# Two changes to a one-core diffusion trunk: the adaLN scale of layer 0 as products on PE, and gate tiles placed behind the key and query projections

## The chip, the cores and the metric

The kernel runs on one core of a Trainium2 chip. The core has five engines with instruction streams of their own: PE (TensorE, matrix products), DVE (VectorE), ACT (ScalarE), POOL (GpSimd) and SP (SyncE, which issues most of the DMA transfers). The metric is the time of one execution on the device in microseconds (us). Three runs of the kernel before took 2922.29, 2915.41 and 2922.88 us, a median of 2922.29 us. The one execution that was profiled took 2915.37 us.

## The reference

The reference is a trunk of two layers over 256 context tokens and 1024 latent tokens of 1024 features (`D`). Each layer mixes tokens and then runs a squared-ReLU MLP. Layer 0 mixes by multi-head latent attention, layer 1 by a bidirectional gated linear attention (GLA). Cut to what the change touches:

```python
m_lat = silu(c)     @ ada_w[i] + ada_b[i]      # 6 rows of D: shift, scale, gate, shift, scale, gate
m_ctx = silu(c_ctx) @ ada_w[i] + ada_b[i]
h_lat = rms_norm(x_lat, norm_g[i, 0]) * (1 + m_lat[1]) + m_lat[0]
h_ctx = rms_norm(x_ctx, norm_g[i, 0]) * (1 + m_ctx[1]) + m_ctx[0]
# layer 0: h_all (context, then latent) goes into
cq, ckv = h_all @ w_dq, h_all @ w_dkv          # low-rank query (384), key/value (256) and rotary key (64)
# layer 1 (GLA): h_all goes into keys, queries, values, a swish gate, and per direction d
g[d] = log_sigmoid((h_all @ w_gate1[d]) @ w_gate2[d] + b_gate[d]) / 16
```

Everything is computed in float32. The kernel gets that accuracy from PE by splitting each operand into a high and a low part and adding three products.

## The kernel before, in words

Features lie on the 128 partitions, tokens along the free dimension. A feature axis of 1024 is eight tiles, `k` = 0 to 7. Tokens form three blocks (`BLK`): 0 is the context (256 tokens), 1 and 2 are latent (512 each). `mm3` (lines 231 to 235) issues the three products of a split pair, so each of the lines 233, 234 and 235 has a third of them. A split (`split`, lines 202 to 204) is a cast on ACT (line 203) and a subtraction on DVE or POOL (line 200).

**Layer 0's inputs** (`low_rank_inputs`). The products of `w_dq` and `w_dkv` form six output tiles per token block, which are accumulated over `k` in six of the eight PSUM banks. `block` runs block 1, then 0, then 2. For block 1 the scale multiplies the weights: `first(k)` computes the latent scale of tile `k` (`ada_lat(1, k)`), scales the weight rows with it on ACT (line 425) and DVE (line 426), and loads the tokens; the tokens are split without a scale. With `ahead`, the work of step `k+1` is issued before the 18 products of step `k`. For block 0 the weights are used unscaled, and `ctx_moving` scales and shifts the tokens (lines 434 to 439), with two more columns that carry the shifts, so that the shift's share (`wb`) of the latent blocks comes out of the same products. Block 2 uses the scaled weights again.

The scale and shift of layer 0 are sums over 1024 features for each of 1024 outputs, for the latent and the context vector. In the kernel before each of the 16 tiles (`m` = 0 shift, `m` = 1 scale, `k` = 0 to 7) has one load of 512 KB into a tile named `ada` with three buffers (outputs on partitions, the 1024 summands along the free dimension). `ada_lat` multiplies it by a row of silu(c), broadcast over partitions in `cs`, and sums, in one DVE instruction (line 396). `ada_ctx` does the same with silu(c_ctx): for the six pairs in `PLAN['dve']` on DVE (line 404), for the other ten with a multiplication on POOL (line 407) and a sum on ACT (line 408). `ada_fix` adds the bias, and for a scale multiplies by the norm's weight: one DVE instruction of one column per sum (line 277 for a shift, line 282 for a scale). `PLAN['post']` and `PLAN['sec']` list what is issued after the products of step `k` of block 1 and block 0: `A` the shift or scale sums, `L` a token load, `S` a square for the norm, `T` the norm's statistics.

**Layer 1's projections** (`gla`). `PLAN['gla']` lists the order in which the items of blocks 2 and 0 run: `v` values, `s` swish gates, `h` keys and queries, `g` decay gates. Each item of `head_proj` is one projection: two weight loads, two splits, 24 products, an ACT copy, a store. `gate_items` first makes one projection of 24 products, copied to SBUF by lines 1290 to 1292; then, for each 128 tokens and each direction, a gate tile:

```python
nc.tensor.matmul(ps, st[:, j * P:j * P + P], self.gs[d], start=True, stop=True)   # 1297
nc.scalar.activation(e, ps, AF.Abs)                                               # 1299
nc.scalar.activation(e, e, AF.Exp, scale=-1.0)                                    # 1300
nc.scalar.activation(e, e, AF.Ln, bias=1.0)                                       # 1301
nc.vector.scalar_tensor_tensor(out=e, in0=ps, scalar=0.0, in1=e, ...)             # 1302
nc.sync.dma_start(self.g_scr[d, t0 // P + j], e)                                  # 1303
```

Blocks 1 and 2 have eight gate tiles, block 0 has four. The gates, keys, queries and values go to scratch in HBM, and the scan reads them back. Block 1's items are not run in `gla`: they are a chain, `fill`, of which the scan takes the next one or few between its own steps (`PLAN['pre']`, `PLAN['fill']`). The scan's first steps are context tiles, then tiles of block 2; block 1's come later. In the scan, line 1450 makes the sums of the gates (fp32 products of 130 columns) and line 1475 loads and splits the values.

**What sets the order.** Each engine runs its instructions in the order of its queue. That order is made at compile time from the program order and a simulated timeline, so an instruction can stand ahead of one that is written before it. DMA loads marked by `keep_in_program_order` (line 378 and others) keep their written order on SP's queue; a load whose buffer is not free yet holds up the queue behind it.

Of the kernel before, what the change touches and what calls it, by code (L numbers as in the profile page):

```python
# [10 lines left out]
F32 = mybir.dt.float32  # L11
F32R = mybir.dt.float32r
U8 = mybir.dt.uint8
AF = mybir.ActivationFunctionType
ALU = mybir.AluOpType
# [30 lines left out]
PLAN = {'dve': [(1, 3), (0, 7), (0, 0), (1, 2), (1, 1), (1, 7)],  # L46
 'sq': [(1, 5), (1, 7), (2, 3), (2, 7), (0, 4), (2, 4), (1, 4), (2, 1), (1, 1)],
 'xlo': [5, 7, 6, 0],
 'wlo': [7, 1, 6, 0],
# [43 lines left out]
 'gla': 'v2 s2 h2 h0 g0 v0 g2',  # L93
# [17 lines left out]
class Trunk:  # L111
    def __init__(self, ctx, tc, I, out, stop=None):
# [7 lines left out]
        def const(name, shape, dt=F32):  # L120
            return self.const.tile(shape, dt, name=name)
# [12 lines left out]
        for l in range(2):  # L134
            for s in range(2):
                for m in range(6):
                    if (l, m) == (0, 0) or l == 1 and s == 1 and m > 1:
                        continue
                    self.coef[l, s, m] = const(f"m{l}{s}{m}", [P, KT])
        self.shift0 = const("shift0", [P, KT, 2])  # L140
        for s in range(2):
            self.coef[0, s, 0] = self.shift0[:, :, s]

# [199 lines left out]
    def lay_out(self, order):  # L343

        for tag in order.split():
            if tag == "cs":
                self.cs = self.pool.tile([P, 2, D], F32, name="cs")
            elif tag == "cl":
                self.cl = self.pool.tile([P, D], F32, name="cl")
            elif tag == "junk":  # L350
                self.junk = self.pool.tile([P, D], F32, name="junk")
            else:
                self.slot(tag, 8)
# [13 lines left out]
    def low_rank_inputs(self):  # L367
# [5 lines left out]
        ada_w = {}  # L373
# [3 lines left out]
        def dma(x, src):  # L377
            self.tc.keep_in_program_order(nc.sync.dma_start(x, src))
            return x
# [14 lines left out]
        def ada_lat(m, k):  # L394
            w = dma(self.slot("ada", D), I["adaT"][0, m * KT + k])
            nc.vector.tensor_tensor_reduce(out=self.junk, in0=w, in1=self.cs[:, 0], scale=1.0, scalar=0.0,
                                           op0=ALU.mult, op1=ALU.add, accum_out=self.co(0, 0, m, k))
            self.ada_fix(0, 0, m, k)
            ada_w[m, k] = w

        def ada_ctx(m, k):
            w = ada_w.pop((m, k))
            if (m, k) in PLAN['dve']:
                nc.vector.tensor_tensor_reduce(out=w, in0=w, in1=self.cs[:, 1], scale=1.0, scalar=0.0,
                                               op0=ALU.mult, op1=ALU.add, accum_out=self.co(0, 1, m, k))
            else:
                nc.gpsimd.tensor_tensor(out=w, in0=w, in1=self.cs[:, 1], op=ALU.mult)
                nc.scalar.activation(w, w, AF.Copy, accum_out=self.co(0, 1, m, k))
            self.ada_fix(0, 1, m, k)

        def ada_lat_ctx(m, k):
            ada_lat(m, k)
            ada_ctx(m, k)
# [93 lines left out]
        def first(k):  # L507
            ada_lat(1, k)
            held[k] = weights(k, self.co(0, 0, 1, k))
            load_x(1, k)  # L510
            return held[k]
# [4 lines left out]
        def second_silu():  # L516
            self.silu(1)
            self.exp_ln_tables()
# [13 lines left out]
        fn = {"A": ada_lat_ctx, "L": load_x, "S": square, "T": stats}  # L532
        self.silu(0)
        post = {k: [(square, 1, k), (ada_ctx, 1, k)] for k in range(KT)}
        post[0].insert(0, (second_silu,))
# [711 lines left out]
    def gla(self, h):  # L1247

        nc, I = self.nc, self.I
        self.gate_weights()  # L1250
        item = {"g": lambda b: self.gate_items(h[b], b), "h": lambda b: self.head_proj(h[b], b),
                "v": lambda b: self.value_items(h[b], b, 4), "s": lambda b: self.swish_items(h[b], b)}
        for x in PLAN["gla"].split():
            b = int(x[1])
            self.ready(h[b])
            self.run(item[x[0]](b))
        x = h[1]
        self.ready(x)
        fill = chain(self.gate_items(x, 1), self.head_proj(x, 1), self.value_items(x, 1, 2), self.swish_items(x, 1))
        return self.scan(fill)  # L1260

# [20 lines left out]
    def gate_items(self, h, b):  # L1282
# [21 lines left out]
        yield  # L1304
# [297 lines left out]
def layout(i):  # L1602
# [5 lines left out]
    A["cb"] = f(np.broadcast_to(np.stack([i["c"][0], i["c_ctx"]])[None], (P, 2, D)))  # L1608
    A["adaT"] = f(i["ada_w"].transpose(0, 2, 1).reshape(2, 48, P, D))
# [53 lines left out]
```

## Time and profile before

| | us |
|---|---|
| median of three runs | 2922.29 |
| the profiled execution | 2915.37 |
| its span, first to last instruction | 2913.6 |
| PE busy in matrix products | 2746.1 (94% of the span) |
| DVE busy | 2313.1 (79%) |
| ACT busy | 1603.9 (55%) |
| POOL busy | 664.0 (23%) |

The page cuts the span into 40 slices of 73 us and gives busy time in tenths, and the clock of PE that the chip granted, in tenths of full speed:

```profile
PE   6799998999989999999999999799888999999997
...
DVE  8898899888788887798868673366898898877666
ACT  4566666666466444444545365656665644545443
...
PEclk8999999999999999999999999899999999999999
```

How to read a profile's row here: durations are in us, or in ns where the view says "mean ns"; `x16` is a count; `128x512` is partitions by elements; `out<-in` are the program's tile names (`m`, `w`, `c`, `ada`, `ps` and so on); `L396` is line 396 of the kernel. "Idle before" is the idle time of the engine just ahead of such instructions, with the instruction that ended it. A matrix product's duration includes its passage through the array, so products in a row start at closer intervals than they last. One fp32 product appears as two records. SPq is the queue in which SP issues DMA transfers.

### The profile page before, as it was taken

How to read it: one execution, taken by the hardware profiler on the slowest of the kernel's cores; microseconds unless marked ns; L12 is line 12 of the kernel's file. 1: busy time of each engine (PE TensorE's matmuls, PEld its weight loads, DVE VectorE, ACT ScalarE, POOL GpSimd, SP SyncE). 2: the span in 40 equal slices, each digit the busy share in tenths (PEclk: the TensorE clock that was granted, in tenths of full speed). 3: DMA queues.
4: the chain of work that ended last, by engine and by line, in shares of the span. 5: the costliest groups of instructions: out<-in, count | busy, mean ns of one | idle time of the engine just before them, and what ended most of it. 6: DMA issues, size and time to landing. Idle time of an engine off the chain costs nothing. (4 is left out here: it accounts for less than half of the span.)

```text
span 2913.6 us, 44354 instructions
## 1 busy us (share of the span) xinstructions
PE 2746.1 (94%) x14646; PEld 2354.7 (81%) x14646; DVE 2313.1 (79%) x4331; ACT 1603.9 (55%) x3360; POOL 664.0 (23%) x474
## 2 busy tenths in 40 slices
PE   6799998999989999999999999799888999999997
PEld 4678887898779888888887888688887778888877
DVE  8898899888788887798868673366898898877666
ACT  4566666666466444444545365656665644545443
POOL 5554444422000000000002233356561000000012
PEclk8999999999999999999999999899999999999999
DMA  5222424313646675498735465666586657677454
GB/s 201 77 77 67 129 94 143 101 61 110 230 124 233 197 250 179 163 342 285 245 122 172 166 222 161 202 218 230 189 275 213 224 195 246 203 269 259 146 178 154
DMA packets 319383, 535.47 MB, mean 184 GB/s; under 512 B 33072, under 2 KB 96432, under 8 KB 319152
## 3 DMA queue, kind: packets, MB, share of 16 engines
q1 hardware_dynamic: 313328, 527.39, 54.5%
q10 hardware_dynamic: 5760, 5.25, 0.5%
q8 instruction: 115, 1.88, 0.3%
q14 instruction: 116, 0.95, 0.1%
q0 software_dynamic: 64, 0.00, 0.0%
HBM read 412.18 MB, written 120.32 MB: 183 GB/s over the span
## 5 line engine op out<-in xcount | busy, mean ns | idle before, releaser
L234 PE MATMUL ps<-m,w 128*128 128x512 f32 (+1 forms) x2320 | 897.5, 388 | 13.2 <-DVE m L200 13.2
L233 PE MATMUL ps<-m,w 128*128 128x512 f32 (+1 forms) x2320 | 882.2, 390 | 25.2 <-ACT m L203 14.5
L235 PE MATMUL ps<-m,w 128*128 128x512 f32 (+1 forms) x2320 | 889.7, 387 | 2.1 <-DVE w L200 2.0
L200 POOL TENSOR_TENSOR w<-stg,w 128x512 fp32r<-128x512 f32 (+2 forms) x138 | 194.1, 1409 | 1706.2 <-ACT w L203 1648.3
L233 PEld LDWEIGHTS ps<-m,w 128*128 128x128 f32 x2320 | 439.4, 190 | 118.8 <-ACT m L203 21.8
L234 PEld LDWEIGHTS ps<-m,w 128*128 128x128 f32 x2320 | 442.0, 191 | 103.8 <-DVE m L200 18.3
L235 PEld LDWEIGHTS ps<-m,w 128*128 128x128 f32 x2320 | 440.1, 190 | 91.6 <-DVE w L200 4.4
L203 ACT CAST w<-stg 128x512 fp32r<-128x512 f32 (+2 forms) x510 | 311.1, 615 | 333.0 <-PE ps L234 247.2
L200 DVE TENSOR_TENSOR w<-stg,w 128x512 fp32r<-128x512 f32 x372 | 273.1, 738 | 142.6 <-ACT w L203 127.8
L203 ACT CAST m<-stg 128x512 fp32r<-128x512 f32 x296 | 177.5, 625 | 141.8 <-DMA stg<-hid 123.6
L233 PE MATMUL ps<-m,m 128*128 128x256 f32 (+1 forms) x632 | 187.9, 316 | 28.7 <-ACT m L203 17.7
L200 DVE TENSOR_TENSOR m<-stg,m 128x512 fp32r<-128x512 f32 x244 | 169.1, 706 | 50.0 <-ACT m L203 49.2
L234 PE MATMUL ps<-m,m 128*128 128x256 f32 (+1 forms) x632 | 198.0, 315 | 7.4 <-DVE m L200 4.1
L233 PE MATMUL ps<-c,w 128*128 128x256 f32 (+1 forms) x664 | 186.9, 288 | 15.8 <-ACT c L435 6.3
L235 PE MATMUL ps<-m,m 128*128 128x256 f32 (+1 forms) x632 | 194.9, 310 | 2.4 <-DVE m L426 2.4
L234 PE MATMUL ps<-c,w 128*128 128x256 f32 (+1 forms) x664 | 185.8, 284 | 5.6 <-DVE c L436 3.5
L235 PE MATMUL ps<-c,w 128*128 128x256 f32 (+1 forms) x664 | 185.1, 284 | 0.6 <-DVE w L200 0.6
L233 PEld LDWEIGHTS ps<-m,m 128*128 128x128 f32 x632 | 124.0, 197 | 39.8 <-ACT m L203 19.7
L203 ACT CAST w<-m 128x512 fp32r<-128x512 f32 x128 | 79.2, 622 | 117.1 <-PE ps L234 116.9
L233 PEld LDWEIGHTS ps<-c,w 128*128 128x128 f32 x664 | 125.7, 192 | 21.2 <-ACT c L435 6.7
L888 DVE TENSOR_TENSOR t<-ps,t 128x512 f32<-128x512 f32 x164 | 111.0, 684 | 37.6 <-PE ps L235 27.1
L234 PEld LDWEIGHTS ps<-m,m 128*128 128x128 f32 x632 | 125.2, 198 | 17.6 <-POOL m L200 5.5
(303 smaller groups left out, 5817.5 us busy)
## 6 DMA issues: line engine op xcount, KB each, us to landing
stg<-in_mlp_w SPq DMA_DIRECT2D x256, 256.0 KB, 4.2
stg<-hid SPq DMA_DIRECT2D x227, 256.0 KB, 3.8
hid<-t SPq DMA_DIRECT2D x205, 256.0 KB, 3.3
stg<-in_w SPq DMA_DIRECT2D x182, 256.0 KB, 3.4
ada<-in_adaT SPq DMA_DIRECT2D x88, 512.0 KB, 3.7
stg<-in_adaT SPq DMA_DIRECT2D x112, 256.0 KB, 4.1
stg<-in_gla_wv SPq DMA_DIRECT2D x64, 256.0 KB, 3.6
stg<-in_mla_wo SPq DMA_DIRECT2D x48, 256.0 KB, 4.4
```

The source lines that it names most:

```text
L200: eng.tensor_tensor(out=out, in0=a, in1=bits(hi), op=ALU.subtract)
L203: self.nc.scalar.copy(hi, src)
L233: mm(ps, lhs[0], rhs[0], start=first, stop=False, skip_group_check=shared)
L234: mm(ps, lhs[0], rhs[1], start=False, stop=False, skip_group_check=shared)
L235: mm(ps, lhs[1], rhs[0], start=False, stop=last, skip_group_check=shared)
L888: eng.tensor_tensor(out=out, in0=a, in1=b, op=op)
```

## The change

The scale and shift of layer 0 get separate functions. `scale(k)` loads the same weights in another layout (`ada0`, summed features on partitions) and forms the sums for the latent and the context vector together: eight fp32 products on PE of 128 x 128 weights with the two columns of silu(c) and silu(c_ctx) (`cc`, a new tile of 128 x 16), accumulated in PSUM, and one DVE instruction for bias and norm weight. `shift(k)` makes both sums on DVE, with one instruction for the bias of both. POOL and ACT take no part in either sum any more. Both broadcast rows `cs` are loaded and go through Silu after step 1 of block 1. `PLAN['post']` and `PLAN['sec']` spread the shifts over steps 2 to 7 of block 1 and steps 0 and 1 of block 0, and load the context tokens from step 2 on.

In layer 1 the gate tiles become separate steps of `gate_items`. A `g` in `PLAN['gla']` now issues the gate projection only, and one gate tile follows each item of the projections behind it. Block 1's tiles go one by one behind its key and query projections in the scan's fill.

```diff
-PLAN = {'dve': [(1, 3), (0, 7), (0, 0), (1, 2), (1, 1), (1, 7)],
...
- 'post': {3: [('A', 0, 0)],
-          4: [('L', 0, 0), ('L', 0, 5), ('S', 0, 0), ('L', 0, 1)],
-          5: [('L', 0, 4), ('L', 0, 2), ('L', 0, 3), ('S', 0, 1), ('S', 0, 2), ('A', 0, 1)],
-          6: [('L', 0, 6), ('L', 0, 7), ('A', 0, 3), ('S', 0, 3), ('S', 0, 4), ('S', 0, 5), ('S', 0, 6),
-              ('S', 0, 7), ('T', 0)],
-          7: [('A', 0, 2), ('A', 0, 4), ('T', 1)]},
- 'sec': {0: [('A', 0, 5)],
-         1: [('L', 2, 0)],
-         2: [],
-         3: [('A', 0, 6)],
+ 'post': {2: [('A', 0), ('L', 0, 0), ('L', 0, 1)],
+          3: [('A', 1), ('L', 0, 2), ('L', 0, 3), ('S', 0, 0), ('S', 0, 1)],
+          4: [('A', 2), ('L', 0, 4), ('L', 0, 5), ('S', 0, 2), ('S', 0, 3)],
+          5: [('A', 3), ('L', 0, 6), ('L', 0, 7), ('S', 0, 4), ('S', 0, 5)],
+          6: [('A', 4), ('S', 0, 6), ('S', 0, 7), ('T', 0)],
+          7: [('A', 5), ('T', 1)]},
+ 'sec': {0: [('A', 6)],
+         1: [('A', 7)],
+         2: [('L', 2, 0)],
          4: [('L', 2, 1)],
-         5: [('A', 0, 7)],
...
- 'gla': 'v2 s2 h2 h0 g0 v0 g2',
+ 'gla': 'v2 s2 g2 h2 g0 h0 v0',
...
+        self.scale0 = const("scale0", [P, KT, 2])
+        self.cc = const("cc", [P, KT, 2])
...
+        def scale(k):
+            w = dma(self.slot("ada", D), I["ada0"][k])
+            ps = self.ps(2)
+            for i in range(KT):
+                nc.tensor.matmul(ps, w[:, i * P:i * P + P], self.cc[:, i], start=i == 0, stop=i == KT - 1)
+            o = KT + k
+            nc.vector.tensor_scalar(out=self.scale0[:, k], in0=ps, scalar1=self.vec1[:, o:o + 1],
+                                    scalar2=self.vec[:, VEC_G + k:VEC_G + k + 1], op0=ALU.add, op1=ALU.mult)
+
+        def shift(k):
+            w = dma(self.slot("ada", D), I["adaT"][0, k])
+            for s, x in enumerate((self.junk, w)):
+                nc.vector.tensor_tensor_reduce(out=x, in0=w, in1=self.cs[:, s], scale=1.0, scalar=0.0,
+                                               op0=ALU.mult, op1=ALU.add, accum_out=self.co(0, s, 0, k))
+            nc.vector.tensor_scalar(out=self.shift0[:, k], in0=self.shift0[:, k], scalar1=self.vec[:, k:k + 1],
+                                    scalar2=None, op0=ALU.add)
...
         def first(k):
-            ada_lat(1, k)
+            scale(k)
...
-        def second_silu():
+        def silus():
+            self.silu(0)
             self.silu(1)
             self.exp_ln_tables()
...
-        self.silu(0)
-        post = {k: [(square, 1, k), (ada_ctx, 1, k)] for k in range(KT)}
-        post[0].insert(0, (second_silu,))
+        dma(self.cc, I["cc"])
+        nc.scalar.activation(self.cc, self.cc, AF.Silu)
+        post = {k: [(square, 1, k)] for k in range(KT)}
+        post[1].append((silus,))
...
+        gates = iter(())
         for x in PLAN["gla"].split():
             b = int(x[1])
             self.ready(h[b])
-            self.run(item[x[0]](b))
+            if x[0] == "g":
+                self.run(gates)
+                gates = item["g"](b)
+                next(gates)
+                continue
+            for _ in item[x[0]](b):
+                self.run_some(gates, 1)
+        self.run(gates)
         x = h[1]
         self.ready(x)
-        fill = chain(self.gate_items(x, 1), self.head_proj(x, 1), self.value_items(x, 1, 2), self.swish_items(x, 1))
+        fill = chain(self.beside(self.head_proj(x, 1), self.gate_items(x, 1)), self.value_items(x, 1, 2),
+                     self.swish_items(x, 1))
         return self.scan(fill)
+
+    @staticmethod
+    def beside(items, others):
+        next(others)
+        yield
+        yield
+        for _ in items:
+            next(others, None)
+            yield
+        Trunk.run(others)
...
                 nc.sync.dma_start(self.g_scr[d, t0 // P + j], e)
-        yield
+                yield
...
+    A["cc"] = f(np.stack([i["c"][0], i["c_ctx"]]).reshape(2, KT, P).transpose(2, 1, 0))
+    A["ada0"] = f(i["ada_w"][0, :, D:2 * D].reshape(KT, P, KT, P).transpose(2, 1, 0, 3).reshape(KT, P, D))
```

## Rows read from the trace of the kernel before

**Rows 1.** Busy time by stretch: us, busy (instructions) by engine, TensorE clock, DMA share, GB/s

```profile
10.70:73.00 62.30, 47.61 (x148) 33.72 (x148) 61.62 (x82) 31.61 (x60) 43.09 (x21) 0.84 0.55 188
73.00:112.40 39.40, 25.06 (x158) 22.59 (x158) 37.78 (x75) 18.11 (x38) 21.02 (x14) 0.83 0.24 85
112.40:230.00 117.60, 107.45 (x569) 87.89 (x568) 103.47 (x186) 81.55 (x187) 62.61 (x46) 1.00 0.22 73
1756.00:1808.00 52.00, 52.00 (x288) 45.45 (x287) 15.99 (x27) 22.93 (x44) 16.03 (x13) 1.00 0.54 165
1808.00:1884.00 76.00, 58.02 (x230) 46.08 (x230) 30.01 (x51) 54.36 (x114) 26.57 (x24) 0.84 0.59 198
```

**Rows 2.** Waits, 5 to 112 us: who waited for whom, us in total, times, longest

```profile
ACT m L425 <- DVE m L282: 23.1, 7, 6.0
...
PE ps L233 <- ACT c L435: 6.3, 1, 6.3
...
PE ps L234 <- DVE c L436: 3.5, 1, 3.5
```

**Rows 3.** Waits of SP's queue, 5 to 112 us

```profile
SPq L378 <- ACT ada L408: 30.3, 7, 8.2
...
SPq L378 <- DVE m L404: 21.7, 4, 6.2
```

**Rows 4.** Groups by shape, PE, 1808 to 1884 us: busy us, mean ns, idle before

```profile
L233 PE MATMUL ps<-m,w 128*128 128x512 f32 x28 | 12.4, 441 | 5.8 <-DVE t L1302 5.8
...
L1297 PE MATMUL ps<-m,m 128*128 128x512 f32 x20 | 6.5, 469 | 6.5 <-DVE m L1292 6.5
```

**Rows 5.** Groups by line, POOL and DVE, 7 to 112 us

```profile
L407 POOL TENSOR_TENSOR ada<-ada,cs 128x1024 f32<-128x1024 f32 x10 | 27.5, 2745 | 20.8 <-ACT cs L357 13.9 <-DVE m L396 2.5 <-DVE c L438 1.8
...
L282 DVE SCALAR_TENSOR_TENSOR m<-m,vec,vec 128x1 f32<-128x1 f32 x16 | 9.4, 595 | 0.0
L277 DVE TENSOR_TENSOR shift<-shift,vec 128x1 f32<-128x1 f32 x16 | 7.5, 480 | 0.0
L404 DVE CUSTOM_DVE_ANT_0 ada<-ada,cs 128x1024 f32<-128x1024 f32 x6 | 7.3, 1213 | 0.2 <-ACT cs L357 0.2
```

**Rows 6.** Timeline, 46 to 51 us: start, duration, line engine operation

```profile
46.47 0.20 DVE L282 SCALAR_TENSOR_TENSOR m<-m,vec,vec 128x1 f32<-128x1 f32 x1
...
48.41 2.33 DVE L282 SCALAR_TENSOR_TENSOR m<-m,vec,vec 128x1 f32<-128x1 f32 x1
...
47.90 2.82 POOL L407 TENSOR_TENSOR ada<-ada,cs 128x1024 f32<-128x1024 f32 x1 [1.37 <-DVE m L396]
```

**Rows 7.** Groups by shape, PE, 0 to 112.4 us

```profile
L234 PE MATMUL ps<-m,m 128*128 128x512 f32 x52 | 23.6, 469 | 4.1 <-DVE m L200 2.2 <-POOL m L200 1.9
```

**Rows 8.** PE: timeline of equal products in a row; then line 1450 with its records

```profile
56.82 1.55 PE L233 MATMUL ps<-m,m 128*128 128x512 f32 x6
...
93.91 0.88 PE L233 MATMUL ps<-c,w 128*128 128x258 f32 x6
...
1861.25 1.05 PE L1450 MATMUL ps<-m,stg 128*128 128x130 f32 x8
...
1872.35 1.24 PE L1450 MATMUL ps<-m,stg 128*128 128x130 f32 x4 [0.32 <-DVE t L1302]
...
L1450 PE MATMUL ps<-m,stg x160: 272/275/586, 1861.3 to 2138.0; 128*128 128x130 f32 x160
```

**Rows 9.** The page's DMA issues: count, size, median us to landing

```profile
ada<-in_adaT SPq DMA_DIRECT2D x88, 512.0 KB, 3.7
```

**Rows 10.** Groups by line, ACT, 1808 to 1884 us

```profile
L1300 ACT ACTIVATE t<-t 128x512 f32<-128x512 f32 x20 | 12.4, 661 | 0.0
...
L1299 ACT ACTIVATE t<-ps 128x512 f32<-128x512 f32 x20 | 11.0, 608 | 1.8 <-PE ps L1297 1.8
```

**Rows 11.** Timeline of SP and ACT, 1835 to 1843 us

```profile
1835.01 1.02 SPq L1361 DMA_DIRECT2D v_scr<-t  x2
...
1842.27 0.62 ACT L203 CAST m<-stg 128x512 fp32r<-128x512 f32 x1 [6.59 <-DMA stg<-v_scr]
```

More of the change, by code (lines that the diff above doesn't have):

```diff
@@ L44 @@
 SCAN_HALVES = (15, 17)
-PLAN = {'dve': [(1, 3), (0, 7), (0, 0), (1, 2), (1, 1), (1, 7)],
- 'sq': [(1, 5), (1, 7), (2, 3), (2, 7), (0, 4), (2, 4), (1, 4), (2, 1), (1, 1)],
+PLAN = {'sq': [(1, 5), (1, 7), (2, 3), (2, 7), (0, 4), (2, 4), (1, 4), (2, 1), (1, 1)],
  'xlo': [5, 7, 6, 0],
  'wlo': [7, 1, 6, 0],
[10 rows of a table removed]
[9 rows of a table added]
          4: [('L', 2, 1)],
[1 row of a table removed]
          6: [('L', 2, 2)],
@@ L136, in __init__ @@
                 for m in range(6):
-                    if (l, m) == (0, 0) or l == 1 and s == 1 and m > 1:
+                    if l == 0 and m < 2 or l == 1 and s == 1 and m > 1:
                         continue
@@ L140, in __init__ @@
         self.shift0 = const("shift0", [P, KT, 2])
+        self.scale0 = const("scale0", [P, KT, 2])
+        self.cc = const("cc", [P, KT, 2])
         for s in range(2):
             self.coef[0, s, 0] = self.shift0[:, :, s]
+            self.coef[0, s, 1] = self.scale0[:, :, s]
         def dram(name, shape):
@@ L347, in lay_out @@
                 self.cs = self.pool.tile([P, 2, D], F32, name="cs")
+            elif tag == "junk":
+                self.junk = self.pool.tile([P, D], F32, name="junk")
             elif tag == "cl":
                 self.cl = self.pool.tile([P, D], F32, name="cl")
-            elif tag == "junk":
-                self.junk = self.pool.tile([P, D], F32, name="junk")
             else:
@@ L372, in low_rank_inputs @@
         gkv = [self.vec[:, VEC_GKV + i:VEC_GKV + i + 1] for i in range(2)]
-        ada_w = {}
         xs, acc, rs, raw, raws, part, held = {}, {}, {}, {}, {}, {}, {}
@@ L392, in stats @@
             rs[b] = self.rstd([acc[b]], BLK[b][1], D)
[L394 to L413, printed above, removed]
+        def scale(k):
[13 more added lines that the diff above has]
+                                    scalar2=None, op0=ALU.add)
         def weights(k, A=None):
@@ L530, in third_moving @@
             return res
-        fn = {"A": ada_lat_ctx, "L": load_x, "S": square, "T": stats}
-        self.silu(0)
-        post = {k: [(square, 1, k), (ada_ctx, 1, k)] for k in range(KT)}
-        post[0].insert(0, (second_silu,))
+        fn = {"A": shift, "L": load_x, "S": square, "T": stats}
+        dma(self.cc, I["cc"])
+        nc.scalar.activation(self.cc, self.cc, AF.Silu)
+        post = {k: [(square, 1, k)] for k in range(KT)}
+        post[1].append((silus,))
         for k, x in ({k: [(fn[a[0]], *a[1:]) for a in x] for k, x in PLAN['post'].items()}).items():
```

## The prediction, made before the changed kernel was run

> **What bounds the kernel now.** PE carries the span, so what is to be had lies where PE is idle or slow. I read the page's slices first, which point to two dips, then busy time by stretch to size them [rows 1]. The reader is to see three kinds of stretch there. From 10.7 to 112.4 us (the first two token blocks of the low-rank input products) PE is busy 73 of 102 us at a granted clock of 0.84, while DVE is busy 99.4 of 102: DVE sets the pace. From 1808 to 1884 us (gate tiles, last value products, start of the scan) PE is busy 58 of 76 us at 0.84, and here no engine is full; ACT comes nearest. In 1756 to 1808 us (key and query projections) PE is never idle and ACT is busy for only 23 of 52 us.
>
> Then the waits. At the start ACT's weight scaling (L425) waits 23.1 us for L282, the last small step of the scale on DVE [rows 2]. SP's queue waits 52 us for slots of the three-buffer `ada` tile, 30.3 of them for L408, the ACT sum behind POOL's context product [rows 3]. In the gate stretch PE waits 6.5 us for the gate projection's copy, and 5.8 us for L1302, the end of the exp/ln chain of a gate tile [rows 4].
>
> **Part 1, the scale of layer 0.** Removed: eight latent products of the scale on DVE (half of L396's sixteen), six context products on DVE (L404), ten on POOL (L407) with their ACT sums (L408), the sixteen L282, and half of the sixteen L277. Added: on DVE eight context products of the shift, and sixteen small operations of 128x2; on PE 64 fp32 products with two columns; one 8 KB load and one small Silu. The sixteen 512 KB loads stay sixteen.
>
> DVE: products fall from 22 to 16, 6 x 1.21 = 7.3 us [rows 5]. Small operations fall from 32 to 16; the undisturbed L282 lasts 0.20 us [rows 6], so some 2 us. The larger term is hidden in long durations: an L282 that starts beside POOL's L407 lasts 2.33 us instead of 0.20 [rows 6], 2.1 us in which DVE stands. L282 averages 595 ns and L277 480 ns for one column [rows 5]. Ten L407 at 2.1 us are 21 us; at the least I count only what L282 and L277 show, 32 operations with 16.9 us busy less 32 x 0.2 = 10 us. I take 18, since DVE hardly ever rests beside an L407 but some of them stop it late. DVE loses 7 + 2 + 18 = 27 us of its 102. From 112.4, where the context block ends now, that makes 85.
>
> PE: 157 products of 512 columns at 0.23 us and 144 of 258 at 0.12 (8 steps of 18 for each block and 13 of the third: lines 233 to 235 have 52 or 53 of the wide ones each, [rows 7]; six in a row give the spacing, [rows 8]) are 36 + 17 = 53 us. The trace has no product of two columns. The nearest is the scan's fp32 L1450, 130 columns: eight records in 1.05 us, 0.13 each with weights loaded anew, and one fp32 product makes two records (20 scan steps with four products show 160) [rows 8]. 64 x 2 x 0.13 = 17 us on PE. Bounds: 0.05 us a record if two columns cost little beside the load (6 us), and 0.31 as in the four records in 1.24 us after a wait (40 us). I take 17. 10 + 53 + 17 = 80: PE's floor is nearly as late as DVE's.
>
> The Trainium skill, "TensorE: Matmul & The Clock Gate", section "LDWEIGHTS (loading the stationary operand)", says that a weight load costs the number of its columns over 1.2 GHz; an estimate from it is 128 x 107 ns = 13.7 us, a floor for PE of 77 instead of 80. The row's 0.13 us a record holds the streaming of 130 columns too, so no row here shows the load alone; the forecast goes by the row.
>
> With floors as close as 80 and 85 us, each engine will wait for the other in turn. At the change from the latent to the context block PE waits 6.3 and 3.5 us for L435 and L436 [rows 2]; of such waits I keep 7.5 us on top of the 85. So 112.4 becomes 92.5: **20 us less**. Ends: 27 with no such wait; 3 if another chain paces the steps (below). The cover for PE's added 17 us is its idle and half-clock time in the stretch, 102 - 53; without it they would come in full.
>
> Waits added: the products of step k+1 stand in PE's queue ahead of the matmuls of step k and wait for a 512 KB load (3.7 us to landing, [rows 9]). Behind them wait the step's matmuls, and SP's later loads (weights and x) wait behind an `ada` load whose slot is not free. Slots free sooner now, after PE's 2 us or DVE's two products, not after POOL and ACT. The Silu rows of 1024 columns move behind step 1, past the third scale's load; the first scale needs only the 8 KB load, worth 1 us. The stretch behind, 112.4 to 230, has PE busy 107 of 118 us, so the gain should be passed on whole.
>
> **Part 2, gate tiles.** The same 20 tiles stay: one product, three ACT passes, one DVE operation, one store each. ACT's passes take 0.61 to 0.66 us [rows 10], 36 us in all, 29 of them for the two blocks of eight tiles that now run as lumps of 14. PE's 230 products in 1808 to 1884 at 0.23 us are 53 us, and 50 if the 28 short ones (scan and transposes) count 0.12: 23 to 26 us of the 76 are lost to idling and the half clock. Twelve tiles move beside block 2's and 0's projections. There ACT goes from 23 to 23 + 12 x 1.8 = 45 us of some 55, still below PE; the weight casts queue behind the passes in ACT's order, for which I set 2 us. In the 256-column block an item has only 2.9 us of PE for a tile's 1.8 of ACT beside two casts and a copy, so that is where they would show. Block 1's eight tiles go beside its eight projections in the scan. SP's stores of gates now stand between weight loads and wait for L1302; the same queue already holds the k and q stores at such places, at no idle PE.
>
> What is late next is the way from the last value products into the scan: v is stored from 1835.0 and its reload lets ACT go on at 1842.3 [rows 11]. Only block 1's gate projection (24 x 0.23 = 5.5 us) and the first scan products stand there to cover it. I leave 7 us lost: the 3 uncovered, the first scores' chain, and some half clock. 26 - 7 - 2 = **17 us less**; ends 0 (the lumps form again) and 25.
>
> **Sum.** 20 + 17 = 37 us from the profiled execution's 2915.4 (span 2913.6) is 2878. The runs shown have that one as their lowest and a median of 2922.3; half the distance more gives **2882**, by which the cases below are placed, from 2919.
>
> **Rivals.**
> *A, gates gain nothing:* the chains fill ACT among the projections, the weight casts come late, and the scan starts with less to do. For: ACT at 80% in order. Against: PE is never idle in 1756 to 1808, with ACT at 44%. 20 us less, 2899.
> *B, the start is paced by slots:* three `ada` buffers, two loads a step. A scale's slot is held 3.7 + 4.1 (behind 18 matmuls) + 2.2 us, a shift's 3.7 + DVE's lag + 2.4; with a lag of 6 (the longest L282 wait, [rows 2]) a step lasts 22/3 = 7.4 us against 62.3/8 = 7.8 now. 3 us less there, 17 in the gates: 2899.
> *C, slower:* the same slots, but SP in order behind a blocked load keeps only two in flight: 22/2 = 11 us a step, 8 x 3.2 = 26 more; less 17, +9: 2928. The time turns to slower once a step exceeds 9.9 us (8 x 2.1 = 17), which is a lag of 3.7. For: SP's 52 us of slot waits. Against: most of these are for L408, which goes.
> *D, it does not do what it says:* the compiler's own order puts tiles and products back where their waits were (a cast for the scan already stands ahead of a gate's copy, [rows 11]), and each part keeps a few us: 2914.
>
> **Chances.** Forecast 0.65, own range 2866 to 2894; A 0.12; B 0.10; D 0.08; C 0.05. Taking 2858 to 2912 leaves out C, most of D, and a little below. A change under 0.3%, 9 us, can't be told from none: faster is forecast, A and B less a tail, 0.85; same 0.09; slower 0.06.
>
> **What would show it.** Right: no POOL L407 or ACT L408 in the first 112 us, DVE's operations of one or two columns near 0.2 us, the context block's last product near 92 us, 128 short PE records there of about 0.13 us; SP's slot waits well under 52 us; between the projections single gate tiles with PE at 100%, and under 10 us of idle PE around the scan's start. Wrong: steps of the first block still 7 us or more, PE waiting for `ada` loads, a lump of exp/ln passes with PE idle, or the two stretches shorter but the time given back in the heads or the scan.

## The result: 2871 us, and the profile after

Four runs of the changed kernel took 2870.07 to 2872.26 us, a median of 2870.9; the kernel before, on the same chip, had a median of 2920.8. The ratio is 0.983 with an interval of 0.982 to 0.985, so 44 to 54 us less. A repeat (experiment 5) gave 0.985 (0.983 to 0.987), 39 to 48 us less. The forecast of 2882 and its range of 2858 to 2912 held. The two spans differ by 43.1 us, 2913.6 to 2870.5, against a forecast of 37.

The page of the kernel after: its span and its 40 slices. Those of the kernel before are in "Time and profile before".

```profile
span 2870.5 us, 44551 instructions
...
PE   8999898999989999999999999999888999999997
...
DVE  6898899887788887798868674476998998777766
ACT  4667576666566444444545456666655645554443
...
PEclk9999999999999999999999999999999999999999
```

In the tenths, both dips of the granted clock are gone, in the first and in the 26th slice. A short one remains inside the second slice (below), and the first slice's figure doesn't show that PE's products ran at half speed up to some 22 us (last section). To place the 43 us I cut every span at the same DMA transfers: the start ends at the first store into `o_scr` (attention's output), "gates and scan" run from the first store into `v_scr` to the last load from `g_scr`. Numbers are us; the last column is when the context block's last product starts. Rows 1 to 10 are the experiments below.

| kernel | start | gates and scan | all else | span | context block |
|---|---|---|---|---|---|
| before | 217.1 | 436.4 | 2260.1 | 2913.6 | 112.2 |
| after | 200.4 | 412.3 | 2257.8 | 2870.5 | 96.5 |
| 1 scale only | 197.5 | 439.8 | 2270.4 | 2907.7 | 93.7 |
| 2 gates only | 217.5 | 414.1 | 2263.7 | 2895.3 | 112.6 |
| 3 all products on DVE | 209.4 | 441.0 | 2253.3 | 2903.7 | 104.2 |
| 4 scale's products twice | 227.2 | 413.8 | 2260.2 | 2901.2 | 122.0 |
| 5 the change again | 201.4 | 413.5 | 2256.9 | 2871.8 | 96.2 |
| 6 shift's products on POOL | 207.3 | 413.8 | 2262.7 | 2883.8 | 103.5 |
| 7 block 1's tiles in a lump | 201.6 | 423.1 | 2256.9 | 2881.6 | 96.4 |
| 8 late shifts on PE | 202.8 | 415.1 | 2262.5 | 2880.4 | 95.7 |
| 9 products ahead | 201.1 | 413.5 | 2261.2 | 2875.8 | 95.9 |
| 10 both 8 and 9 | 205.9 | 417.5 | 2257.3 | 2880.7 | 98.4 |

The start gave 16.7 us and the gates and scan 24.1; the rest, which no edit touches, gave 2.3, and lies anywhere from 2253 to 2270 in the twelve profiles. A single profile's span is therefore not read more closely than some 8 us. Its stretches repeat better: the start takes 197.5 to 201.6 in the four kernels that share the change's first part (after, 1, 5, 7), the gates and scan 412 to 418 in the eight that share its second.

**The start.** Busy time by stretch, first of the kernel after, then of the kernel before. The columns are: the stretch, its length, busy us (instructions) of PE, PE's weight loads, DVE, ACT and POOL, then the granted clock, the DMA share and GB/s.

```profile
10.70:96.50 85.80, 76.90 (x412) 66.40 (x412) 68.31 (x130) 40.69 (x80) 29.57 (x24) 0.94 0.53 179
96.50:200.40 103.90, 95.79 (x480) 77.45 (x479) 91.07 (x163) 73.39 (x166) 58.21 (x42) 0.98 0.22 72
67.00:80.00 13.00, 7.19 (x26) 6.21 (x27) 13.00 (x32) 5.03 (x11) 2.47 (x3) 0.62 0.00 0
70.80:76.00 5.20, 3.19 (x10) 2.33 (x11) 5.20 (x13) 3.10 (x7) 1.46 (x1) 0.50 0.00 0
```

```profile
10.70:112.20 101.50, 72.47 (x304) 56.11 (x305) 99.31 (x155) 49.51 (x97) 64.10 (x34) 0.83 0.43 148
112.20:217.10 104.90, 94.75 (x479) 76.03 (x478) 91.86 (x163) 73.43 (x166) 56.83 (x42) 1.00 0.22 74
```

DVE was busy 99 of 102 us and is busy 68 of 86: it has lost 31 us and no longer sets the pace alone. PE now has 77 of 86. What follows the context block takes 104 us against 105, so the gain is passed on whole. PE's timeline after shows who paces what: start, duration, products in a row, and the idle time before them.

```profile
5.59 3.54 PE L398 MATMUL ps<-cc,ada 128*128 128x2 f32 x16 [5.59 <-DMA ada<-in_ada]
9.87 3.58 PE L398 MATMUL ps<-cc,ada 128*128 128x2 f32 x16 [0.74 <-DMA ada<-in_ada]
13.30 2.91 PE L233 MATMUL ps<-m,m 128*128 128x512 f32 x6
...
27.61 1.84 PE L398 MATMUL ps<-cc,ada 128*128 128x2 f32 x16
29.31 1.19 PE L233 MATMUL ps<-m,m 128*128 128x512 f32 x4
...
33.54 1.84 PE L398 MATMUL ps<-cc,ada 128*128 128x2 f32 x16
...
39.46 1.84 PE L398 MATMUL ps<-cc,ada 128*128 128x2 f32 x16
...
45.39 1.84 PE L398 MATMUL ps<-cc,ada 128*128 128x2 f32 x16
...
66.58 0.39 PE L235 MATMUL ps<-m,m 128*128 128x512 f32 x1
70.81 0.80 PE L233 MATMUL ps<-c,w 128*128 128x258 f32 x2 [3.84 <-ACT c L431]
72.92 0.58 PE L234 MATMUL ps<-c,w 128*128 128x258 f32 x1 [1.31 <-DVE c L432]
...
96.50 0.28 PE L235 MATMUL ps<-c,w 128*128 128x258 f32 x1
```

From 27.61 to 45.39 us a step is 5.93 us: one scale takes 1.70 (27.61 to 29.31) and its 18 wide products 4.23 (29.31 to 33.54). PE is never idle there; it paces. At the turn from block 1 to the context block it waits 3.8 and 1.3 us. DVE has no gap from 55.3 us on: eight of its sixteen shift products stand between 55.3 and 68.7, and the scaling of the context tokens (L430), for which ACT's L431 and then PE wait, comes behind them at 69.74. PE's granted clock is 0.62 from 67 to 80, and 0.50 in the part from 70.8 to 76.

```profile
55.32 1.23 DVE L406 CUSTOM_DVE_ANT_0 junk<-ada,cs 128x1024 f32<-128x1024 f32 x1 [0.55 <-DMA ada<-in_adaT]
...
67.53 1.22 DVE L406 CUSTOM_DVE_ANT_0 ada<-ada,cs 128x1024 f32<-128x1024 f32 x1
...
69.74 2.06 DVE L430 SCALAR_TENSOR_TENSOR t<-k,scale,c 128x256 f32<-128x256 f32 x5
```

DVE's groups of the start, and the waits of SP's queue from 0 to 100 us, after:

```profile
L406 DVE CUSTOM_DVE_ANT_0 junk<-ada,cs 128x1024 f32<-128x1024 f32 x8 | 12.0, 1502 | 1.4 <-DMA ada<-in_adaT 1.3
L406 DVE CUSTOM_DVE_ANT_0 ada<-ada,cs 128x1024 f32<-128x1024 f32 x8 | 11.1, 1384 | 0.1
...
L408 DVE TENSOR_SCALAR shift<-shift,vec 128x2 f32<-128x2 f32 x8 | 2.5, 312 | 0.1
L400 DVE TENSOR_SCALAR scale<-ps,vec,vec 128x2 f32<-128x2 f32 x8 | 2.2, 274 | 6.6 <-PE ps L398 6.5
```

```profile
SPq L377 <- DVE shift L406: 10.8, 3, 4.1
SPq L377 <- DVE shift L408: 9.4, 2, 4.8
SPq L377 <- PE ps L398: 7.3, 2, 5.2
```

DVE's small operations, L408 and L400, average 0.31 and 0.27 us; those that they replace averaged 0.48 and 0.60 [rows 5]. SP waits 27.5 us for `ada` slots (the three rows together) instead of 52 [rows 3].

**Gates and scan.** Busy time of the kernel after over its last projections, gate tiles and the scan's start, then of the kernel before at the same place (a stretch of like length, not the same count of products). Below them stand PE's one idle place after and, a little ahead of it, ACT's wait for the reload of v:

```profile
1740.00:1870.00 130.00, 128.44 (x656) 109.25 (x655) 58.29 (x95) 87.21 (x178) 54.34 (x44) 1.00 0.65 215
```

```profile
1756.00:1890.00 134.00, 116.02 (x550) 96.75 (x550) 47.98 (x81) 79.70 (x163) 44.06 (x37) 0.91 0.58 188
```

```profile
1828.04 0.62 ACT L203 CAST m<-stg 128x512 fp32r<-128x512 f32 x1 [5.03 <-DMA stg<-v_scr]
...
1831.18 0.44 PE L1506 MATMUL ps<-ident,c 128*128 128x128 f32 x2 [1.56 <-POOL c L886]
```

Before, PE was idle for 18 of 134 us, at a granted clock of 0.91; after, for 1.56 of 130 at 1.00. ACT is busy 87 of the 130 us, and no wait of PE in this stretch ends with it.

### The profile page after: what moved, and what is told of

Read it like the earlier page. It is cut to its first block, busy times and chain, and to the rows that moved or that the text cites. A ratio compares the mean times of both kernels' runs of the same rounds, so it can differ in the third digit from the quotient of the medians.

```text
span 2870.5 us, 44551 instructions
## 1 busy us (share of the span) xinstructions
PE 2747.0 (96%) x14774; PEld 2362.8 (82%) x14774; DVE 2280.4 (79%) x4303; ACT 1594.9 (56%) x3341; POOL 638.2 (22%) x464
## 4 chain that ended last, share of the span: by engine, by line
PE 75%; DVE 14%; ACT 4%; DMA 4%; issue 2%; POOL 1%; SPq 0%; DVEq 0%; ACTq 0%; POOLq 0%
PE ps L234 23%; PE ps L233 23%; PE ps L235 22%; DVE m L200 2%; PE ps L736 1%; DVE y L709 1%; DVE ada L252 1%; DMA stg<-hid 1%; PE ps L704 1%; ACT m L203 1%; PE ps L705 1%; PE ps L706 1%; PE ps L707 1%; PE ps L708 1%; PE ps L308 1%
## 5 line engine op out<-in xcount | busy, mean ns | idle before, releaser
L233 PEld LDWEIGHTS ps<-m,w 128*128 128x128 f32 x2320 | 438.2, 190 | 111.9 <-ACT m L203 23.1
L233 PEld LDWEIGHTS ps<-m,m 128*128 128x128 f32 x632 | 124.1, 198 | 22.6 <-DVE m L1531 7.7
L965 ACT ACTIVATE t<-t 128x512 f32<-128x512 f32 x109 | 68.7, 631 | 127.0 <-DVE t L886 120.2
```

Source lines behind the costliest of these rows:

```text
L233: mm(ps, lhs[0], rhs[0], start=first, stop=False, skip_group_check=shared)
L965: self.nc.scalar.activation(c, c, AF.Relu)
```

## Experiments

All were timed beside the kernel before. Ratios are of the medians, with a 95% interval. Expectations stand as written before each run.

**1. Scale only** and **2. gates only.** Each part of the change without the other (1: `'gla': 'v2 s2 h2 h0 g0 v0 g2'`, the old `gate_items` and the old `fill`; 2: the old `low_rank_inputs` and its `PLAN` entries).

> Part 1 alone (scale as products on PE, shifts on DVE; gates as before). Theory: the two stretches are separate and each gain is passed on whole, so the context block's last product falls near 97 us (112.4 before, 96.6 with both parts) and the time is 15 to 17 us below before, ratio 0.9945. Rival: the parts help each other, or the changed order elsewhere gives a share of the 43 us by itself; then this kernel and the one with the gates alone do not sum to the change, and this one gains under 10 or over 22 us.

> Part 2 alone (gate tiles behind the projections; scale as before). Theory: 24 to 26 us below before, ratio 0.9915, PE idle in the gate stretch under 3 us, the start as before (112.4 us). Rival: as in the run of part 1 alone; the two do not sum to the change of both.

Scale only: 2909.5 us, ratio 0.9963 (0.9951 to 0.9975), 7 to 14 us less. Gates only: 2895.4 us, ratio 0.9908 (0.9892 to 0.9925), 22 to 32 us less. Each changes its own stretch as the whole change does (start 197.5 and 217.5, gates and scan 439.8 and 414.1). The gates alone came out as expected; the scale alone shortened the start by 19.6 us, but the whole time by less than the 15 to 17 that I expected. By the ratios the parts give some 38 us, the change 44 to 49; the intervals overlap (29 to 46 for the sum of the parts, 39 to 54 for the change). The stretches show no interaction: the scale-only kernel's start is even 2.9 us shorter than the change's, a lead that it has by its fourth scale (24.30 us against 27.61), since its third ran at full speed (14 records in 1.81 us against 2.98). Its gates and scan are 3 us longer than those of the kernel before and its untouched rest 10, which takes up what the total lacks. Why a given program has a longer rest stays open; none of its steps was edited. No run takes either part apart further: the new order of loads and Silu rows is in the first part with the products, the new order in `PLAN['gla']` in the second with the spreading.

**3. All context products on DVE.** Only this in the kernel before:

```diff
-            if (m, k) in PLAN['dve']:
+            if True:
```

> The kernel before, with all sixteen context products of the scale and shift on DVE, none on POOL and ACT. Theory: POOL's 1024-column products stop DVE for about 2.1 us each, more than the 1.2 us that the same product takes on DVE; ten fewer stops are worth 21 us against 12 us of added DVE work, so the start gets 5 to 12 us shorter although the engine that is full gets more to do. Rival: DVE's long small operations have another cause, and the ten products add their 12 us to a full engine: 8 to 13 us slower.

2911.1 us, ratio 0.9965 (0.9953 to 0.9978), 6 to 14 us less. The start is 7.7 us shorter, as expected, though DVE got ten more products. Its rows for the start:

```profile
10.70:104.20 93.50, 66.51 (x303) 52.34 (x304) 89.97 (x176) 38.70 (x78) 34.37 (x24) 0.87 0.48 163
```

```profile
L404 DVE CUSTOM_DVE_ANT_0 ada<-ada,cs 128x1024 f32<-128x1024 f32 x16 | 19.3, 1212 | 0.2 <-ACT cs L357 0.2
L282 DVE SCALAR_TENSOR_TENSOR m<-m,vec,vec 128x1 f32<-128x1 f32 x16 | 7.3, 460 | 0.0
```

L404 took 7.3 us for six [rows 5] and takes 19.3 for sixteen, 12.0 more; yet DVE's busy time falls from 99.3 to 90.0. So 21.3 us of what looked like DVE's work vanish with ten POOL products: 2.1 each, as the long L282 beside an L407 said [rows 6]. Only about 5 of the 21 us are in L282 and L277; the rest is spread over DVE's other operations. The L282 still average 460 ns, while POOL still makes its splits. In [rows 6] the long L282 ends at 50.74 us and the L407 beside it at 50.72. The Trainium skill ("SBUF — State Buffer", section "SBUF: two separate sides") has DVE and GpSimd share one pair of ports as a lock held for a whole instruction; these rows agree.

**4. The scale's products twice.** Each scale's eight products are issued twice. The second eight start the sum anew, so the value stays and only PE's work doubles:

```diff
-            for i in range(KT):
+            for i in 2 * tuple(range(KT)):
```

> The changed kernel with every fp32 product of the scale made twice (64 more, 128 more records). Theory: the steps of block 1 are now paced by PE (5.94 us a step = 18 x 0.228 + 1.84), so each step grows by 1.84 us and the two first by 3.5: 15 to 18 us more than the changed kernel, ratio to before 0.9885 or so. Rival: DVE still sets the pace, PE has slack, and the time grows by under 5 us.

2901.7 us, ratio 0.9935 (0.9921 to 0.9949). The start is 26.8 us longer than the change's, more than the 15 to 18 that I expected. PE's group of these products, and two of its steps:

```profile
L398 PE MATMUL ps<-cc,ada 128*128 128x2 f32 x256 | 36.7, 279 | 5.5 <-DMA ada<-in_ada 5.5
...
36.86 3.63 PE L398 MATMUL ps<-cc,ada 128*128 128x2 f32 x32
...
44.58 3.63 PE L398 MATMUL ps<-cc,ada 128*128 128x2 f32 x32
```

A step without other waits lasts 7.7 us instead of 5.9 (36.86 to 44.58), so the 1.8 us added to it come in full: PE has no cover left in these steps, and DVE, which got no work, does not pace them. In all the products go from 19.6 us busy to 36.7, 17 more. The path grew by 10 more than that. The granted clock is lower there (0.85 from 10.7 us to the end of the context block, against 0.94 in the change), but how the 10 us divide was not taken apart.

**5. The change again**, the same kernel a second time, to see whether 43 us is scatter.

> The changed kernel, unaltered, a second time, beside the others of this set. The two parts alone gained 10.8 and 26.9 us in all runs (9.6 and 23.7 by their medians against before), 33 to 38 together, where both gave 50. Theory: by stretches the parts do add up (start 16.7 to 19.6, gates 22 to 24), and what is over is scatter of single executions in stretches that neither part touches; the change then comes out at 38 to 45 us below before this time. Rival: the parts help each other; it comes out at 48 to 50 us again.

2874.4 us, ratio 0.985 (0.9834 to 0.9865). It came out as expected. Start and gates are within 1.2 us of the first profile: the gain is the change's, not scatter.

**6. The shift's context products back on POOL.** In the change:

```diff
+            nc.gpsimd.tensor_tensor(out=w, in0=w, in1=self.cs[:, 1], op=ALU.mult)
+            nc.scalar.activation(w, w, AF.Copy, accum_out=self.co(0, 1, 0, k))
```

in place of the second of `shift`'s two DVE products.

> The changed kernel, with the eight context products of the shift on POOL with their sums on ACT, as ten were before. Theory: each stops DVE for 2.1 us and takes only 1.2 us off it, so DVE loses 7 us; part of that hides behind PE, which paces steps 2 to 5 of block 1, the rest falls on the turn from block 1 to block 0, where DVE is full: 2 to 7 us slower than the changed kernel, the context block's last product at 99 to 104 us (96.6). Rival: an engine that is idle for 20 us there (POOL) takes work off a full one: 3 to 9 us faster.

2881.7 us, ratio 0.9882 (0.9867 to 0.9897), slower than the change (0.985); the context block ends 7 us later. POOL's product and the bias behind it on DVE, busy time by stretch, and two DVE operations at the turn:

```profile
L407 POOL TENSOR_TENSOR ada<-ada,cs 128x1024 f32<-128x1024 f32 x8 | 21.2, 2652 | 6.5 <-PE ps L235 2.2 <-DVE shift L409 1.8 <-DVE shift L405 1.3
...
L409 DVE TENSOR_SCALAR shift<-shift,vec 128x2 f32<-128x2 f32 x8 | 5.3, 666 | 0.2 <-ACT ada L408 0.2
...
10.70:103.50 92.80, 79.82 (x409) 69.33 (x410) 63.70 (x114) 49.16 (x96) 50.57 (x32) 0.89 0.48 168
...
65.95 5.98 POOL L407 TENSOR_TENSOR ada<-ada,cs 128x1024 f32<-128x1024 f32 x2 [2.16 <-PE ps L235]
67.09 2.31 DVE L409 TENSOR_SCALAR shift<-shift,vec 128x2 f32<-128x2 f32 x1
...
69.76 2.46 DVE L318 TENSOR_TENSOR c<-c,c 128x256 f32<-128x256 f32 x1
```

The time is near the expected range, but the way there is not what I wrote. DVE was to be busy 7 us more; it is busy 4.6 us less (63.7 against 68.3). Eight products and the reading of their sums took 11.7 us off it, so a POOL product stopped it for some 0.9 us on average here (an estimate from these two figures), not 2.1. The loss shows at the turn, where DVE is full: beside two POOL products from 65.95 to 71.93 a bias lasts 2.31 us and a norm operation 2.46, L431 (the change's L430) starts at 72.72 instead of 69.74, and PE's first product of the context block comes at 73.79 instead of 70.81. An idle POOL is no free place for such a product when it falls on a full DVE.

**7. Block 1's gate tiles in a lump**, ahead of its key and query projections in the scan's fill:

```diff
-        fill = chain(self.beside(self.head_proj(x, 1), self.gate_items(x, 1)), ...
+        fill = chain(self.together(self.gate_items(x, 1)), self.head_proj(x, 1), ...
```

where `together` runs all eight tiles as one item.

> The changed kernel, but block 1's eight gate tiles run as one lump in the scan's fill, as before, ahead of its projections; blocks 2 and 0 stay spread. Theory: the lump brings back its own idle time, which before was 5.6 us of waits in the scan's first products and some 3 us at half clock behind it: 7 to 10 us slower than the changed kernel, so that 15 us of the gain belong to blocks 2 and 0. Rival: the stall needs the two lumps in succession and the late values; one lump alone is hidden by the scan's own products: under 2 us.

2884.4 us, ratio 0.9887 (0.9873 to 0.9902), slower by 10 us, as expected; gates and scan take 423.1 us instead of 413. What PE waits for from 1820 to 1850 us is again the chain's end:

```profile
PE ps L1475 <- DVE t L1327: 7.7, 2, 7.4
```

So the place of block 1's tiles accounts for 10 of the 24 us, and the new order of blocks 2 and 0 for the other 13 or 14.

**8. The last four shifts as products on PE** (a layout as the scale's, one DVE operation), to empty DVE at the turn.

> The changed kernel, with the shifts of tiles 4 to 7 also as products on PE (their weights loaded in the layout of the scale's), the first four on DVE as they are. Theory: from 54 to 80 us DVE is full, with eight of these products (9.2 us) in it, and PE waits 8 us and runs at half clock; 32 more products cost PE 4 x 1.84 = 7.4 us, some of it in the steps that PE paces: 2 to 6 us faster than the changed kernel. Rival: PE paces this stretch as well, and the products come in full: 4 to 8 us slower.

2882.5 us, ratio 0.9876 (0.9857 to 0.9896), 8 us slower than the change by the medians, though the intervals overlap. The turn's wait for L431 goes, the first product there comes at 69.4 us instead of 70.8, and the block's last still starts at 95.7. Busy time from the first wide product to the block's last, in this kernel and in the change:

```profile
13.30:95.70 82.40, 77.16 (x452) 68.41 (x452) 51.83 (x109) 38.72 (x75) 29.81 (x24) 0.98 0.51 174
```

```profile
13.30:96.50 83.20, 74.30 (x400) 63.80 (x400) 65.96 (x126) 38.51 (x75) 29.57 (x24) 0.94 0.51 173
```

DVE has 14 us less and nothing comes of it: my expectation was wrong. What its relief gave back to PE (idle time 5.2 us instead of 8.9, and a higher granted clock) the 32 added products took (four times 1.84 us). The rival's 4 to 8 us more in this stretch did not show either; most of the 8 us lie in the untouched rest (2262.5 against 2256.9 in experiment 5), which no run explains.

**9. Two products of 512 columns ahead of the first scale**, their result not used, and **10. with the late shifts on PE as well.**

```diff
+        nc.vector.memset(self.junk[:, :512], 1.0)
+        for _ in range(2):
+            nc.tensor.matmul(self.ps(), self.ident, self.junk[:, :512], start=True, stop=True)
```

> The changed kernel with two fp32 products of 512 columns of ones issued on PE ahead of the first scale; their result is not used. In the changed kernel PE is idle to 5.6 us, the first two scales' products last 3.5 us each at half clock (1.84 later, at full clock) and the first wide products come at half clock too. Theory that this low clock is a cost of the start: the first two scales take 1.8 to 3 us each, the first wide product comes 1 to 4 us earlier, the context block ends 1 to 4 us earlier, and the kernel gains 1 to 4 us. Rival that PE's clock is low there for want of busy PE just then, whatever came earlier: the first two scales stay at 3.5 us and the time is that of the changed kernel within 2 us. Rival that DVE sets this part: the first wide product comes earlier, and the context block still ends at 96 us.

> The same two products ahead, and the last four shifts of layer 0 as products on PE, as the scales are. Alone the shifts on PE ended the context block at 95.7 us against 96.2 to 96.5 for the change. Theory that PE and DVE pace the start by turns, so that relief of one alone does little: with both, the context block ends at 90 to 93 us and the kernel gains 3 to 6 us over the change. Rival that PE alone paces it now: the context block ends at 94 to 96 us, and the time is that of the change within 3 us.

Nine: 2876.5 us, ratio 0.9867 (0.9848 to 0.9886), which holds the change's 0.985: no gain. Ten: 2882.5, ratio 0.9884 (0.9862 to 0.9905), no gain either, and the context block ended at 98.4 us, later than theory and rival had it. PE's first products in nine, and the granted clock there:

```profile
5.75 2.07 PE L398 MATMUL ps<-cc,ada 128*128 128x2 f32 x16 [0.32 <-DMA ada<-in_ada]
9.72 3.57 PE L398 MATMUL ps<-cc,ada 128*128 128x2 f32 x16 [1.91 <-DMA ada<-in_ada]
13.39 2.93 PE L233 MATMUL ps<-m,m 128*128 128x512 f32 x6
```

```profile
9.20:13.30 4.10, 3.57 (x16) 3.48 (x16) 2.14 (x4) 2.94 (x6) 0.00 (x0) 0.53 1.08 399
```

The first scale is faster (2.07 us against 3.54), the second waits 1.9 us for its load and is at half clock again, and the first wide product comes no earlier. Its fourth scale, at 24.89 us, is 2.7 us ahead of the change, and the context block ends 0.6 us earlier: the lead is lost at the turn (PE waits 4.8 us for L431 there). That the two products brought this lead is not shown. Ten has the same two ahead, and its first scale takes 3.54 us and its fourth starts at 28.74; scale only has none ahead, and its fourth starts at 24.30. In ten, the granted clock was low in another place, 0.78 from 67 to 90 us. The theory that relieving both at once would give 3 to 6 us did not hold; with the clock differing between the two kernels, this doesn't show what the rest is worth at full clock.

No kernel here is faster than the change.

## Why the prediction was right, and where its terms were off

**What bounds.** Right: two stretches, both gains in them, nothing given back. Rival A fell with experiment 2 (22 to 32 us from the gates alone). B and C fell with the slots: SP waits 27.5 us and the steps are 5.93 us, not 7.4 or 11. D fell, since both parts gave most of what they were to give.

**DVE's 27 us.** Measured 31 (99.3 to 68.3). The 7 us of products went by 1.21 us each; they average 1.4 before and after, and in this stretch fell from 28.7 to 23.1 us, 5.6 less. The 18 chosen for POOL's products was a choice between 10 and 21, and experiment 3 puts it at 21.

**PE's 17 us.** Measured 19.6 busy, for two reasons that pull apart. I had divided L1450's 1.05 us by eight. Read from start to start, as I read the wide products, that row gives (1.05 - 0.27) / 7 = 0.11 us a record, and 14 us in all. At full speed a scale does take 1.70 us, 0.106 a record (27.61 to 29.31). But the first three scales ran at half speed (3.54, 3.58 and some 3.3 us), for which I had no term. The Trainium skill's rule ("TensorE: Matmul & The Clock Gate", section "LDWEIGHTS (loading the stationary operand)") gave 0.107 a load; the full-speed rows agree with it.

**Waits of 7.5 us: the term that failed.** With DVE at 31 less, its floor was 81, and the block ended at 96.5, not 92.5: 15 us above the floor, twice the 7.5. DVE is idle 17.5 us in the stretch (85.8 - 68.3) against 2.2 before. Seen from PE, the first wide product starts at 13.30, and of the 83.2 us from there to 96.50 PE is idle for 8.9 and loses some 8.5 to half speed (an estimate from the spacing of its products up to 23.3 us and from 70.8 to 81.5). Without these two it would have been done at 79, so my floor of 80 for PE was about right, and what lies above it I had priced too low.

Both causes stand in the program order that I had read. The first wide product was to come 1 us earlier and came 2.6 later, since `ahead` puts the second scale's products in PE's queue ahead of step 0. They start when their 512 KB load has landed, at 9.87, and take 3.58 us at half speed; I had named that queue and set no price. Then half of the shifts are bunched between 55 and 69 us: PE waits behind them at the turn and runs at half clock after that wait (0.50 from 70.8 to 76). Experiment 4 shows PE as the pace of the steps, and experiment 8 that neither engine alone paces the whole.

That the start came within 4 us of the forecast is in part luck: DVE's term was 4 us too small and the waits 7.5 us too small, and the two errors have opposite signs.

**Gates, 17 us.** Measured 24. Of the 26 us lost before I left 7 for the start of the scan and 2 for ACT. About 1.6 us of idle PE remain, and no wait of PE ends with ACT's passes. The reload of v is still late and ACT waits 5 us for it, but PE has other work for all but 1.6 us, and the clock stays at 1.00. One reading was off without effect: in 1808 to 1884 us the busiest engine was PE itself (58 us), not ACT (54).

**The sum.** 3 us too much at the start, 7 too little in the gates, 2 elsewhere: 43 for 37. That is 6 of the 11 us from 2882 to 2871. The others are the choice of a base: I placed the cases from 2919, 3.6 above the profiled run of the kernel before, and the changed kernel's median lies 1.4 below its own profiled run.

## What to carry to other kernels

When DVE looks full, check what its short instructions cost beside a POOL instruction before moving work to POOL: in the kernel before, ten POOL products cost DVE as much time as some seventeen of its own. In the change eight cost it less than they took off, and the time still rose, because two fell where DVE was full. When the floors of two engines come out within 5 us, as here, allow for more waits than the idle time seen now, and look at the first step and at the turn between blocks, where the new work stands ahead of old work in a queue. Spread chains like exp/ln over work that leaves ACT idle: block 1's eight tiles in a row cost 10 us here, one at a time behind projections nothing that PE's waits show.

## What the runs showed of the hardware

The granted clock can read 1.00 where products run at half speed. In the change the six wide products at 13.30 us took 2.91 us under a reading of 1.00; in experiment 9 the same six took 2.93 under 0.50. At full speed six such products took 1.55 us [rows 8]. So in these traces durations tell more than the column, up to the first change that it shows.

The start's half speed did not end at the same place in each kernel. In the change PE issued two-column products from 5.6 to 9.1 and from 9.9 to 13.3 us, then six wide ones, and the third scale at 16.0 us was still at the slow rate (14 records in 2.98 us). Behind the same six wide products it took 1.71 us in experiment 9 and 1.81 in experiment 1, and 2.98 again in experiment 10. What decided between them these runs don't show; it was worth some 3 us at the fourth scale's start.

A POOL product's price for DVE is not one number. The ten of 128x1024 cost it 2.1 us each in the kernel before, where DVE was busy 99 of 102 us, and eight of them some 0.9 each in experiment 6, where it was busy 64 of 93.
